# Cosine attention on one core: a third chunk of exponentials made off ScalarE, V cast for four pairs at once, twelve Q sums on TensorE, values of three pairs summed by chunk

## The chip, the cores and the metric

The kernel runs on 1 core of one Trainium2 chip. The metric is device time in microseconds (us) of one execution; lower is better. Before the change the median of 3 runs is 188.96 us (188.9 to 189.21).

## What is computed

Q, K and V have 8 batches, 12 heads, 512 rows and 64 columns, in float32; tau is 0.1.

```python
Q_norm = Q / (np.linalg.norm(Q, axis=-1, keepdims=True) + 1e-10)
K_norm = K / (np.linalg.norm(K, axis=-1, keepdims=True) + 1e-10)
scores = np.einsum('bhqd,bhkd->bhqk', Q_norm, K_norm) / tau
weights = np.exp(scores - np.max(scores, axis=-1, keepdims=True))
weights = weights / (np.sum(weights, axis=-1, keepdims=True) + 1e-10)
return np.einsum('bhqk,bhkd->bhqd', weights, V).astype(np.float32)
```

The scores lie between -10 and 10, so the kernel takes the exponentials without subtracting the maximum; the quotient is the same.

## The kernel before

The 96 heads are worked off as 48 **pairs** of heads, numbered s = 0 to 47. The 512 keys of a head are cut into 4 **chunks** c of 128. For each pair the work goes like this:

- SP (the DMA queue) loads Q, K (L311) and V (L314) into rings of buffers and stores the output (L565).
- POOL squares Q and K (L337, `sq`). The squares are summed over the 64 columns in one of two ways. For K of most pairs PE multiplies them by an identity in eight matmuls that add up in the columns 320 to 383 of an output bank (L354, op `SSQ`), and DVE reduces the 64 columns that are left to 8 (L361). For Q, and for K of pairs 35, 39, 43 and 47, DVE reduces all 512 columns (L365). Which way is taken follows from `BY_VECTOR` and `Q_ON_PE` (L626, L627) in `on_pe`.
- DVE makes 1/norm of a group of pairs by Newton steps on small tiles (L389 to L403, op `NEW`); groups have 1, 2 and, from pair 20 on, 4 pairs.
- Q is scaled on DVE, K on POOL or, for the pairs in `K_ON_DVE` (L628), on DVE (both L420, op `SCL`).
- PE transposes the scaled tiles into one PSUM tile (L426, `TR`), and DVE copies it to SBUF (L434, `EVA`). The next pair's transposes wait for that copy.
- For each chunk PE makes the scores of both heads, 128 keys by 512 queries each (L508, `SCO`), in one of two halves of the score tile `scps`, and ScalarE takes the exponential of both heads in one instruction of 1024 elements (L531, `EXP`). The scores of a chunk wait for the exponential of the chunk two before it, which read the same half.
- POOL casts V to bf16 (L536, `VC`) into `vb`, which has a 65th column of ones, so that the value matmuls give the sum of the weights too.
- PE multiplies the exponentials with V, 4 matmuls for each of 4 query tiles and 2 heads (L548, `PV`), into one bank per head; DVE takes the reciprocal of the sums (L559, `RCP`) and multiplies (L561, `NRM`). A bank is free for the next pair's values when that is done, and when the sum of squares that borrowed the bank has been reduced (`bank_free`).

Two chunks do without ScalarE: chunk 3 of pairs 37 and 45 (`OFF`, L617). Their Q scales get another factor (L411), PE makes the scores in the transposes' tile (L468, `SCX`), and a polynomial does the rest: per head two DVE steps (L473, L475), then on 1024 elements four POOL steps (L479, L480) and two DVE steps (L486, L480).

Every instruction is an `Op` with a due time and a list of what it needs. The order in which an engine issues its operations isn't made in the kernel: `ORDER` (L654 to L746) is a list of numbers for each engine, each the place at which the operation was added. Each engine is served strictly in that order, and an operation that waits holds up all behind it on its engine. `RINGS` (L631) gives the number of buffers, in this order: Q/K, V, squares, scaled tiles, transposed tiles, exponentials, outputs, norms.

The last pair (`last`, L567) is cut finer: its chunk 3 has three exponentials, and its values are made chunk by chunk (L576) in three pieces.

Of the kernel before, what the change touches and what calls it, by code (L numbers as in the profile page):

```python
# [19 lines left out]
class Program:  # L20
# [5 lines left out]
    def add(self, key, eng, kind, due, needs, emit, **kw):  # L26
        assert key not in self.ops, key
        op = Op(key, eng, kind, due, needs, emit, **kw)
        self.ops[key] = op
        self.list.append(op)  # L30
        return op

# [76 lines left out]
def bass_cosine_similarity_attention_kernel(  # L109
# [10 lines left out]
    NT = SEQ // 128  # L120
# [9 lines left out]
    qk = [sb(f"qk{i}", [128, 2, 2, NT * DIM], f32) for i in range(R_QK)]  # L130
    vf = [sb(f"vf{i}", [128, 2, NT * DIM], f32) for i in range(R_V)]
    vb = sb("vb", [128, R_QK, NT, 2, DIM + 1], bf16)
    sq = [sb(f"sq{i}", [128, 16, DIM], bf16) for i in range(R_SQ)]
    qn = [sb(f"qn{i}", [128, 2, NT, 2, DIM], bf16) for i in range(R_QN)]
# [16 lines left out]
    o_ps = [nc.alloc_psum_tensor(f"ops{b}", [128, 512], f32) for b in range(2)]  # L151
# [25 lines left out]
    def key(name, s, *rest):  # L177
# [9 lines left out]
        vb[:, :, :, :, DIM : DIM + 1].rearrange("p r c h o -> p (r c h o)"), 1.0))  # L187
# [25 lines left out]
    for s, w in sorted(((s, w) for s in range(NP) for w in range(2) if on_pe(s, w)), key=lambda j: (due_red(j[0]), j)):  # L213
# [12 lines left out]
    for s in range(NP):  # L226
        for h in range(2):
            bank_free[s, h] = before[h]
            before[h] = [("NRM", s, h)] + ([("RED",) + attached[s, h]] if (s, h) in attached else [])
# [67 lines left out]
    def pair(s):  # L297
# [6 lines left out]
        for w, x in ((0, Q), (1, K)):  # L304
            if s == 0:
# [8 lines left out]
              lambda e: e.dma_start(out=vf[iv][:, :, :], in_=src(V, s)), slot=f"v{iv}")  # L314
# [99 lines left out]
        for w in range(2):  # L414
# [3 lines left out]
            P.add(("SCL", s, w), "dve" if dve else "pool", "sclq" if dve else "sclk", T0 - (2.85 if w and not dve else 2.55) - slack(s, M_SCL),  # L418
                  [("NEW", g, (7 if direct_r(g) else 6) if acts and dve else 6 + w + (dve and w))] + ([("UNIT", s)] if s in off_of and w == 0 else []) + ([("TR", 0, w, 0), ("TR", 0, w, 1)] if s == R_QN else [key("TR", s - R_QN, w)]),
                  lambda e, w=w, r=r: e.tensor_tensor(  # L420
                      out=qn[iqn][:, w].rearrange("p t h d -> p h t d"),
                      in0=qk[iq][:, w].rearrange("p h (t d) -> p h t d", t=NT), in1=r, op=ALU.mult))
# [71 lines left out]
    def rest(s):  # L494
# [3 lines left out]
        for c in range(NT):  # L498
# [26 lines left out]
            for hs in ((0,), (1,)) if s == 0 and c < 2 else ((0, 1),):  # L525
# [9 lines left out]
        P.add(("VC", s), "pool", "vc", T0 + 3.0 - slack(s, M_VC), [("LV", s), key("PV", s - R_QK, 0, NT - 1), key("PV", s - R_QK, 1, NT - 1), "vone"],  # L535
              lambda e: e.tensor_scalar(  # L536
                  out=vb[:, iq, :, :, 0:DIM].rearrange("p c h d -> p h c d"),
                  in0=vf[iv][:, :, :].rearrange("p h (c d) -> p h c d", c=NT),
                  scalar1=1.0, scalar2=1.0, op0=ALU.mult, op1=ALU.mult))
# [3 lines left out]
        for h in range(2):  # L543
            for i in range(NT):
                def pv(e, h=h, i=i):
                    for c in range(NT):
                        t = i
                        last = e.matmul(  # L548
                            out=o_ps[h][:, 65 * t : 65 * t + 65],
                            lhsT=et[iet][:, c, h, 128 * t : 128 * t + 128], rhs=vb[:, iq, c, h, :],  # L550
                            start=(c == 0), stop=(c == NT - 1))
                    return last

                need, due = sum((exps(s, c) for c in range(NT)), []), T0 + PERIOD + 0.9 * PV_AT[4 * h + i] + late(s)
                P.add(("PV", s, h, i), "pe", "pv", due, need + [("VC", s)] + (bank_free[s, h] if i == 0 else [("PV", s, h, i - 1)]), pv)
            grid = o_ps[h][:, 0 : 65 * NT].rearrange("p (t x) -> p t x", x=65)
            P.add(("RCP", s, h), "dve", "rcp", T0 + PERIOD + 0.9 * PV_AT[4 * h + 3] + late(s),
                  [("PV", s, h, NT - 1), ("SSQ",) + attached[s, h] if (s, h) in attached else None, key("NRM", s - R_O, h)],
                  lambda e, h=h, grid=grid: e.reciprocal(out=rd[io][:, h, :], in_=grid[:, :, DIM]))  # L559
            P.add(("NRM", s, h), "dve", "nrm", T0 + PERIOD + 0.2 + 0.9 * PV_AT[4 * h + 3] + late(s), [("RCP", s, h), key("ST", s - R_O)],  # L560
                  lambda e, h=h, grid=grid: e.tensor_tensor(  # L561
                      out=ob[io][:, h], in0=grid[:, :, 0:DIM],
                      in1=rd[io][:, h, :].unsqueeze(2).to_broadcast([128, NT, DIM]), op=ALU.mult))
# [3 lines left out]
    def last(s, T0):  # L567
        iq, iet, io = s % R_QK, s % R_ET, s % R_O
        spare = t_ps[:, :, :, :].rearrange("p w t x -> p (w t x)").bitcast(f32)
        for k, (h, lo, hi) in enumerate(PIECES):  # L570
            bank = spare if k == 2 else o_ps[h]
            for c in range(NT):
                def pv(e, h=h, lo=lo, hi=hi, c=c, bank=bank):
                    for t in range(lo, hi):
# [3 lines left out]
                            rhs=vb[:, iq, c, h, :], start=(c == 0 and t == lo), stop=(c == NT - 1), skip_group_check=True)  # L578
                    return last

                op = P.add(("PV", s, k, c), "pe", "pv" if hi - lo == NT else "pvh", T0 + 0.9 * c + 2.5 + 0.1 * k,
                           [("EXP", s, c, k) if c == NT - 1 else ("EXP", s, c), ("VC", s)]
                           + (([("EVA", s)] if k == 2 else bank_free[s, h]) if c == 0 else [("PV", s, k, c - 1)]), pv)
# [33 lines left out]
OFF = {(45, 3): ((45, 45), False), (37, 3): ((37, 37), False)}  # L617
# [7 lines left out]
PE_BOTH = 4  # L625
BY_VECTOR = (35, 39, 43, 47)  # L626
Q_ON_PE = ()  # L627
K_ON_DVE = (1, 2, 3, 4, 9, 15, 21, 27, 33, 39, 40)  # L628
# [151 lines left out]
```

## Time and profile before

| | |
|---|---|
| median of 3 runs | 188.96 us (188.9 to 189.21) |
| the profiled execution | 188.88 us, span 187.0 us, granted clock 0.996 |
| HBM read, written | 37.75 MB, 12.58 MB |

The span reaches from the first to the last instruction. The costliest groups are these; the number after x is the count, then come busy time in us, the mean time of one in ns, and the engine's idle time just before them:

| line, engine | what | count | busy us | mean ns |
|---|---|---|---|---|
| L531 ACT | exponential, 128x1024 | 187 | 171.9 | 1168 |
| L337 POOL | squares, 128x1024 | 44 | 82.8 | 1897 |
| L508 PE | scores, 64x512 | 380 | 74.9 | 386 |
| L548 PE | values, 128x65 | 1504 | 73.7 | 194 |
| L561 DVE | output | 94 | 38.6 | 417 |
| L420 DVE | scale, 128x512 | 58 | 38.4 | 675 |
| L420 POOL | scale, 128x512 | 36 | 37.3 | 1046 |
| L426 PE | transposes | 376 | 33.8 | 220 |
| L434 DVE | copy of the transposed pair | 47 | 32.1 | 683 |
| L365 DVE | sums of squares, 512 to 8 | 48 | 32.1 | 681 |
| L536 POOL | cast of V, 128x512 | 48 | 31.0 | 659 |
| L354 PE | sums of squares, 128x64 | 368 | 18.2 | 193 |
| L361 DVE | the rest of these sums, 64 to 8 | 40 | 8.5 | 215 |

Records of neighbours overlap on PE, ACT, DVE and POOL, so count times mean is more than the busy time: the pace of an engine is read from the distance between two starts.

### The profile page before, as it was taken

To read this page: it belongs to the slowest core of one execution; us is meant where nothing else is said; L and a number is where in the kernel's file an instruction comes from. 1 tells how busy PE (TensorE), PEld (TensorE's weight loads), DVE (VectorE), ACT (ScalarE), POOL (GpSimd) and SP (SyncE) were. 2 spreads that over 40 slices of the span, in tenths; PEclk is the share of its full clock that TensorE was granted. 3 is DMA by queue.
4 is the path that set the end of the run, shared out by engine and by line. 5 is a ranking of instruction groups with operands and counts; after the bars stand their busy time and mean duration, and the time that the engine had idled before them with its cause. 6 is when DMAs were issued, how large, how long until landed. Compare 5 with 4: busy or idle time off the path is not lost.

```text
span 187.0 us, 6631 instructions
## 1 busy us (share of the span) xinstructions
PE 173.1 (93%) x2694; PEld 108.3 (58%) x2694; DVE 172.5 (92%) x545; ACT 181.0 (97%) x214; POOL 166.8 (89%) x152
## 2 busy tenths in 40 slices
PE   6898999999999999999999999899999989999983
PEld 2555666566565665666555555566565556656652
DVE  2789999999999999999999999999999999989863
ACT  4899999999999999999999999999999999999994
POOL 4797999999999999999999999999999999796600
PEclk9999999999999999999999999999999999999998
DMA  5999999899999998899999999896997551303315
GB/s 172 339 357 352 348 357 321 279 322 344 379 378 377 330 325 269 274 336 277 359 381 380 380 361 296 272 274 206 293 297 247 176 168 60 110 6 112 116 60 170
DMA packets 52446, 50.76 MB, mean 272 GB/s; under 512 B 3136, under 2 KB 52416, under 8 KB 52416
## 3 DMA queue, kind: packets, MB, share of 16 engines
q1 hardware_dynamic: 51984, 50.02, 81.6%
q8 instruction: 21, 0.34, 0.7%
q10 hardware_dynamic: 432, 0.33, 0.5%
q14 instruction: 9, 0.07, 0.1%
HBM read 37.75 MB, written 12.58 MB: 269 GB/s over the span
## 4 chain that ended last, share of the span: by engine, by line
ACT 92%; DMA 2%; PE 2%; SPq 1%; issue 1%; DVE 0%
ACT et L531 91%; DMA qk<-in_Q_dram 2%; PE ops L548 1%; PE ops L576 1%; PE scps L508 1%; SPq L311 0%; SPq L308 0%; ACT ys L379 0%; DVE ob L598 0%; ACT sq L329 0%; ACT nps L382 0%; PE tps L576 0%; DVE rd L587 0%
## 5 line engine op out<-in xcount | busy, mean ns | idle before, releaser
L531 ACT ACTIVATE et<-scps 128x1024 bf16<-128x1024 f32 (+1 forms) x191 | 174.0, 1155 | 0.0
L337 POOL TENSOR_TENSOR sq<-qk 128x1024 bf16<-128x1024 f32 x44 | 82.8, 1897 | 1.4 <-DMA qk<-in_K_dram 0.9
L508 PE MATMUL scps<-qt 64*128 64x512 bf16 x380 | 74.9, 386 | 8.0 <-ACT et L531 5.1
L548 PE MATMUL ops<-vb,et 128*128 128x65 bf16 x1504 | 73.7, 194 | 0.3 <-ACT et L531 0.3
L548 PEld LDWEIGHTS ops<-vb,et 128*128 128x128 bf16 x1504 | 55.9, 98 | 28.2 <-issue 20.2
L561 DVE TENSOR_TENSOR ob<-ops,rd 128x256 f32<-128x256 f32 x94 | 38.6, 417 | 0.5
L420 DVE TENSOR_TENSOR qn<-qk,nps 128x512 bf16<-128x512 f32 x58 | 38.4, 675 | 0.4 <-ACT nps L382 0.4
L420 POOL TENSOR_TENSOR qn<-qk,rk 128x512 bf16<-128x512 f32 x36 | 37.3, 1046 | 1.3 <-DVE rk L394 1.1
L508 PEld LDWEIGHTS scps<-qt 64*128 64x128 bf16 x380 | 18.8, 92 | 26.9 <-ACT et L531 14.0
L426 PE MATMUL tps<-ident,qn 128*128 128x128 bf16 x376 | 33.8, 220 | 0.4 <-POOL qn L420 0.2
L434 DVE COPY qt<-tps 128x1024 bf16<-128x1024 bf16 x47 | 32.1, 683 | 1.7 <-PE tps L426 1.4
L365 DVE TENSOR_REDUCE nps<-sq 128x8 f32<-128x512 bf16 x48 | 32.1, 681 | 0.0
L536 POOL TENSOR_SCALAR vb<-vf 128x512 bf16<-128x512 f32 x48 | 31.0, 659 | 0.2
L426 PEld LDWEIGHTS tps<-ident,qn 128*128 128x128 bf16 x376 | 21.5, 98 | 11.3 <-issue 5.7
L354 PE MATMUL ops<-sq,ident 128*128 128x64 bf16 x368 | 18.2, 193 | 0.0
L559 DVE RECIPROCAL rd<-ops 128x4 f32<-128x4 f32 x94 | 15.6, 172 | 2.7 <-PE ops L548 2.2
L354 PEld LDWEIGHTS ops<-sq,ident 128*128 128x128 bf16 x368 | 13.7, 98 | 3.6 <-issue 2.7
L361 DVE TENSOR_REDUCE nps<-ops 128x8 f32<-128x64 f32 x40 | 8.5, 215 | 0.3 <-PE ops L354 0.2
L390 DVE SCALAR_TENSOR_TENSOR nps<-nps,ys 128x32 f32<-128x32 f32 (+1 forms) x30 | 6.3, 209 | 0.3
L389 DVE TENSOR_TENSOR nps<-nps,ys 128x32 f32<-128x32 f32 (+1 forms) x30 | 6.2, 207 | 0.2
L480 POOL TENSOR_TENSOR xz<-xz 128x1024 f32<-128x1024 f32 x2 | 3.8, 1894 | 2.1 <-DVE xz L475 2.1
L191 PE MATMUL ops<-warm_in,ident 128*128 128x512 bf16 x8 | 3.5, 615 | 1.4 <-POOL ident L181 1.4
(62 smaller groups left out, 63.6 us busy)
## 6 DMA issues: line engine op xcount, KB each, us to landing
vf<-in_V_dram SPq DMA_DIRECT2D x48, 256.0 KB, 5.7
qk<-in_Q_dram SPq DMA_DIRECT2D x47, 256.0 KB, 4.5
qk<-in_K_dram SPq DMA_DIRECT2D x47, 256.0 KB, 5.6
out_dram<-ob SPq DMA_DIRECT2D x47, 256.0 KB, 3.6
qk<-in_Q_dram SPq DMA_DIRECT2D x2, 128.0 KB, 2.7
qk<-in_K_dram ACTq DMA_DIRECT2D x2, 128.0 KB, 3.0
out_dram<-ob SPq DMA_DIRECT2D x1, 128.0 KB, 1.7
out_dram<-ob ACTq DMA_DIRECT2D x1, 64.0 KB, 1.7
```

The costliest lines, as they stand in the source:

```text
L337: lambda e: e.tensor_tensor(out=sqf, in0=data, in1=data, op=ALU.mult))
L354: last = e.matmul(out=o_ps[bank][:, 320:384], lhsT=ident[:, :], rhs=sq[iqs][:, 8 * w : 8 * w + 8, 8 * k : 8 * k + 8], start=(k == 0), stop ...
L365: lambda e, w=w, dst=dst: e.tensor_reduce(out=dst, in_=sq[iqs][:, 8 * w : 8 * w + 8, :], axis=AX.X, op=ALU.add))
L420: lambda e, w=w, r=r: e.tensor_tensor(out=qn[iqn][:, w].rearrange("p t h d -> p h t d"), in0=qk[iq][:, w].rearrange("p h (t d) -> p h t d" ...
L426: last = e.transpose(t_ps[:, w, t, :], qn[iqn][:, w, t].rearrange("p h d -> p (h d)"), ident[:, :])
L434: lambda e: e.tensor_copy(out=qt[iqt][:, :, :, :].rearrange("p w t x -> p (w t x)"), in_=t_ps[:, :, :, :].rearrange("p w t x -> p (w t x)")))
L508: last = e.matmul(out=sc_ps[:, 2 * b + h, :], lhsT=qt[iqt][64 * h : 64 * h + 64, 1, c, :], rhs=qt[iqt][64 * h : 64 * h + 64, 0, :, :], sta ...
L531: lambda e, c=c, b=b, hs=hs: e.activation(out=et[iet][:, c, hs[0] : hs[-1] + 1, :], in_=sc_ps[:, 2 * b + hs[0] : 2 * b + hs[-1] + 1, :], f ...
L536: lambda e: e.tensor_scalar(out=vb[:, iq, :, :, 0:DIM].rearrange("p c h d -> p h c d"), in0=vf[iv][:, :, :].rearrange("p h (c d) -> p h c ...
L548: last = e.matmul(out=o_ps[h][:, 65 * t : 65 * t + 65], lhsT=et[iet][:, c, h, 128 * t : 128 * t + 128], rhs=vb[:, iq, c, h, :], start=(c = ...
L559: lambda e, h=h, grid=grid: e.reciprocal(out=rd[io][:, h, :], in_=grid[:, :, DIM]))
L561: lambda e, h=h, grid=grid: e.tensor_tensor(out=ob[io][:, h], in0=grid[:, :, 0:DIM], in1=rd[io][:, h, :].unsqueeze(2).to_broadcast([128, N ...
```

## The change

- `OFF` gets chunk 3 of pair 31: it leaves ScalarE and takes the way of pairs 37 and 45.
- The value matmuls of pairs 45, 37 and 31 (`BY_CHUNK`) are ordered by chunk: each `PV` operation takes one chunk for all four query tiles, the off-engine chunk last, in place of one query tile with all four chunks. The values of pairs 37 and 31 take their banks after those of the next pair (`LATER`).
- V is laid out by head, then chunk, and cast for several pairs in one instruction: pairs 8 to 15 two by two, pairs 16 to 47 four by four (`JOINT`, `join`); pairs 0 to 7 stay single.
- The Q sums of squares of the even pairs 24 to 46 go to PE (`Q_ON_PE`).
- K of pairs 23, 24, 26, 28 and 30 is scaled on DVE, K of pair 40 on POOL again (`K_ON_DVE`).
- The rings for Q/K, V, scaled tiles and outputs change from 15, 10, 4, 8 to 16, 12, 6, 6.
- All of `ORDER` is new. ScalarE's list only loses the one exponential. In the new list of PE, 8 value matmuls stand between the scores of chunks 1 and 2 of pair 47, and 32 between those of chunks 2 and 3. The stores of pairs 31 and up stand behind the last load in SP's list.

The code also gets forms for joint scales, reciprocals and outputs, which `JOINT` doesn't name; they are cut here, as is `ORDER`.

```diff
+    def join(self, name, members, eng, kind, due, needs, emit, *rest):
+
+        op = self.add((name, members[-1]) + rest, eng, kind, due, needs, emit)
+        for s in members[:-1]:
+            self.ops[(name, s) + rest] = op
...
-    vf = [sb(f"vf{i}", [128, 2, NT * DIM], f32) for i in range(R_V)]
-    vb = sb("vb", [128, R_QK, NT, 2, DIM + 1], bf16)
+    vf = sb("vf", [128, R_V, 2, NT * DIM], f32)
+    vb = sb("vb", [128, R_QK, 2, NT, DIM + 1], bf16)
...
-    for s in range(NP):
+    for s in sorted(range(NP), key=lambda i: i + (1.5 if i in LATER else 0)):
         for h in range(2):
             bank_free[s, h] = before[h]
...
-        P.add(("VC", s), "pool", "vc", T0 + 3.0 - slack(s, M_VC), [("LV", s), key("PV", s - R_QK, 0, NT - 1), key("PV", s - R_QK, 1, NT - 1), "vone"],
-              lambda e: e.tensor_scalar(
-                  out=vb[:, iq, :, :, 0:DIM].rearrange("p c h d -> p h c d"),
-                  in0=vf[iv][:, :, :].rearrange("p h (c d) -> p h c d", c=NT),
-                  scalar1=1.0, scalar2=1.0, op0=ALU.mult, op1=ALU.mult))
+        wide = {4: "v4", 2: "v"}
+        last_of = [n for n in wide if (s, wide[n]) in JOINT]
+        both = [s - i for i in range(last_of[0] - 1, -1, -1)] if last_of else [s]
+        if last_of or not any((s + i, wide[n]) in JOINT for n in wide for i in range(1, n)):
+            P.join("VC", both, "pool", {1: "vc", 2: "vc2", 4: "vc4"}[len(both)], T0 + 3.0 - slack(s, M_VC),
+                   [("LV", i) for i in both] + [key("PV", i - R_QK, h, NT - 1) for i in both for h in range(2)] + ["vone"],
+                   lambda e: e.tensor_scalar(
+                       out=vb[:, iq + 1 - len(both) : iq + 1, :, :, 0:DIM].rearrange("p r h c d -> p (r h c) d"),
+                       in0=vf[:, iv + 1 - len(both) : iv + 1].rearrange("p r h (c d) -> p (r h c) d", c=NT),
+                       scalar1=1.0, scalar2=1.0, op0=ALU.mult, op1=ALU.mult))
...
                     for c in range(NT):
                         t = i
+                        if s in BY_CHUNK:
+                            t, c = c, last_chunk[i]
                         last = e.matmul(
                             out=o_ps[h][:, 65 * t : 65 * t + 65],
-                            lhsT=et[iet][:, c, h, 128 * t : 128 * t + 128], rhs=vb[:, iq, c, h, :],
-                            start=(c == 0), stop=(c == NT - 1))
+                            lhsT=et[iet][:, c, h, 128 * t : 128 * t + 128], rhs=vb[:, iq, h, c, :],
+                            start=(i == 0 and t == 0) if s in BY_CHUNK else c == 0,
+                            stop=(i == NT - 1) if s in BY_CHUNK else c == NT - 1, skip_group_check=s in BY_CHUNK)
...
-OFF = {(45, 3): ((45, 45), False), (37, 3): ((37, 37), False)}
+OFF = {(37, 3): ((37, 37), False), (45, 3): ((45, 45), False), (31, 3): ((31, 31), False)}
...
+LATER = (37, 31)
+BY_CHUNK = (45, 37, 31)
+JOINT = ((11, 'v'), (13, 'v'), (15, 'v'), (19, 'v4'), (23, 'v4'), (27, 'v4'), (31, 'v4'), (35, 'v4'), (39, 'v4'), (43, 'v4'), (47, 'v4'), (9, 'v'))
 BY_VECTOR = (35, 39, 43, 47)
-Q_ON_PE = ()
-K_ON_DVE = (1, 2, 3, 4, 9, 15, 21, 27, 33, 39, 40)
+Q_ON_PE = (24, 26, 28, 30, 32, 34, 36, 38, 40, 42, 44, 46)
+K_ON_DVE = (1, 2, 3, 4, 9, 15, 21, 23, 24, 26, 27, 28, 30, 33, 39)
 VLAG = 3
 LATE, LATE_TO = 0.0, 10
-RINGS = 15, 10, 6, 4, 4, 4, 8, 3
+RINGS = 16, 12, 6, 6, 4, 4, 6, 3
```

## The prediction, made before the changed kernel ran

> **What bounds the kernel now.** I read the busy line of the page first, then the busy time by stretch, then the chain that ended last, then the waits of each engine, and at last the timeline of PE.
>
> ```profile
> PE 173.1 (93%) x2694; PEld 108.3 (58%) x2694; DVE 172.5 (92%) x545; ACT 181.0 (97%) x214; POOL 166.8 (89%) x152
> ```
> ```profile
> 14.00:88.00 74.00, 71.51 (x1169) 45.95 (x1168) 72.40 (x250) 74.00 (x83) 72.91 (x64) 1.00 1.01 331
> 88.00:172.00 84.00, 78.71 (x1224) 48.70 (x1219) 81.96 (x247) 83.98 (x93) 80.00 (x69) 1.00 0.75 244
> 172.00:187.00 15.00, 11.42 (x200) 7.60 (x198) 9.58 (x28) 12.21 (x17) 3.82 (x3) 0.95 0.35 116
> ```
>
> The columns of the second fence are window, length, then busy time of PE, PEld, DVE, ACT, POOL, the granted clock and the DMA. ScalarE never rests between 14 and 172 us. But DVE has only 2.0 us free in the 84 us from 88 on, PE 5.3 and POOL 4.0: all four engines are close to full where the change works (pairs 23 to 47).
>
> ```profile
> 14.77 149.41 ACT et L531 x163
> ...
> 179.94 0.39 PE scps L508 x2
> 180.33 0.84 PE ops L548 x24
> 181.17 0.32 PE scps L508 x2
> 181.50 0.59 PE ops L548 x16
> 182.09 0.32 PE scps L508 x2
> ```
>
> The chain is exponentials, one after another, and only the last 4 us go through PE. 149.41 over 163 is 0.917 us for one. In the trace's single records most starts lie 0.90 to 0.91 apart (median 0.904) though the row says 1.17 for each: neighbours overlap. The starts that are later than 0.904 add up to 2.3 us in the run. So ScalarE does stall a little, in gaps too short to be counted as idle; the place to see why is PE's timeline, where L508 makes the scores that an exponential reads:
>
> ```profile
> 155.12 0.39 PE L508 MATMUL scps<-qt 64*128 64x512 bf16 x2
> 155.44 0.66 PE L548 MATMUL ops<-vb,et 128*128 128x65 bf16 x16
> 155.93 0.40 PE L354 MATMUL ops<-sq,ident 128*128 128x64 bf16 x8
> 156.26 0.39 PE L508 MATMUL scps<-qt 64*128 64x512 bf16 x2
> ```
>
> Two score steps should be 0.904 apart; here 16 value matmuls and 8 sums of squares stand between them and they are 1.14 apart, and the exponential after them starts 1.10 after the one before it. A second kind of stall is a wait for data. Of those two matter late in the run: a transpose on PE that waited 0.23 for a scale on POOL (the exponential came 0.26 late) and value matmuls that waited 0.30 for an exponential (0.14 late).
>
> ```profile
> PE ops L548 <- ACT et L531: 0.3, 1, 0.3
> PE tps L426 <- POOL qn L420: 0.2, 1, 0.2
> ```
>
> **The change, part by part.** The profiled execution took 188.88 us with a span of 187.0 (1.9 around it, taken as fixed); the median of the runs is 188.96. The sum is made against 188.88. Durations are start to start of neighbouring records where the engine didn't wait.
>
> *ScalarE.* One exponential less (pair 31, chunk 3): -0.90.
>
> *DVE.* The chunk needs four steps of 0.61 (L473, L475), one of 1.15 (L486), one of 0.61 (L480) and a small one (L411, 0.1): +4.3. K scales move here for pairs 23, 24, 26, 28, 30 and leave for 40: four times 0.595 = +2.4. Twelve Q sums become L361 reductions of 0.131 in place of L365's 0.593: -5.5. Net +1.2. It isn't spread evenly: up to pair 34 it is +3.0 (five scales) +4.3 -2.8 (six sums) = +4.5, and it comes back later. What hides it is DVE's lead: the copy of the transposed pair (L434) ends 0.9 to 7 us before the pair's first exponential. In the new order list the work ahead of that copy grows by 1.9 for pair 34 (lead now 4.1), by 0.3 for pair 40 (lead 0.9). With ScalarE 0.9 earlier, pair 40's is 0.3 late. I take +0.2; ends 0 and +1.4 (rival C).
>
> *POOL.* The chunk: two steps of 1.85 and two of 1.0, +5.7. Four scales of 1.005 go: -4.0. Casts of V: 48 become 8 single, 4 double, 8 fourfold, so 28 instructions go. What a fourfold cast takes no row shows. The fixed part of a POOL instruction can be worked out from rows: squares start 1.852 apart at 1024 elements (L337) and 1.003 at 512 (L331), so 0.155 doesn't scale; 28 times that is -4.4. The ends are 0 and, if a cast of 2048 went as fast as one of 512 (0.585), -16; I take -4.4, from the nearest row. Net -2.7. POOL isn't what ScalarE waits for, but the wait of 0.23 above goes: the K scale of pair 43 has 2.9 us less work ahead of it. The gap with the 0.30 wait is filled in another way. Together -0.4 (0.26 and 0.14); ends 0 and -0.6.
>
> *PE.* Twelve times eight sums of squares, 29 ns apart: 12 times 0.232 = 2.8 us of work, beside the 5.3 us free from 88 on. That it fits in total isn't enough: it must fit between score steps. A score step takes 0.319, and the first one after other matmuls starts 0.126 after the last of them, where these follow each other in 0.030 (L548), 0.029 (L354) or 0.056 (L426). So a gap has room for 0.904 - 0.319 - 0.126 = 0.46 us. I counted the other work in each gap of both lists (four value matmuls 0.12, four transposes 0.224, eight sums 0.232). Up to the last pair, gaps with 0.68 us or more: 7 before, spread over the run; 17 after, all from pair 24 on. The 7 cost 0.48 now (0.05, 0.09, 0.04, 0.20, 0.12, and two nothing), 0.07 each. Ten more at 0.07 are +0.7; at 0.12, as they now come close behind each other and lateness is carried over, +1.2; at nothing, 0. I take +0.8.
>
> The 0.126 agrees with the Trainium skill, TensorEngine Tiling (Array Packing), Key Properties: changing the tiling mode drains TensorE; the trace has it at both ends of every score step (64 rows against 128).
>
> *The tail.* Now 24 value matmuls stand before the scores of chunk 2 of pair 47 and 16 before chunk 3; the latter start 2.1 us after those of chunk 1. In the new list it is 8 and 32: chunk 2's scores must wait 0.9 for their bank, then 0.319 + 0.97 + 0.126 follow: 2.3. +0.2; ends 0 and +0.3.
>
> *Values by chunk, larger rings, loads.* By-chunk sums are as many matmuls with other starts, and let pair 31's wait for its off-engine chunk alone. SP issues the same loads, and rings of 16 and 12 let them start earlier; stores of pairs 31 to 47 queue behind the last loads, and a ring of 6 needs the store of pair s before the output of s+6, some 20 us later. 0, hidden by a lead of POOL's squares of over 20 us; without that cover each load costs its 4.5 to 5.7 us to landing.
>
> **Sum:** -0.90 + 0.2 - 0.4 + 0.8 + 0.2 = -0.1: 188.8 us.
>
> **Rivals.**
>
> B, PE has the room. Crowded gaps cost little because PE catches up in light ones (two of the 7 cost nothing). For: 5.3 us free. Against: a lost start can't be won back, as ScalarE has no slack. -0.90 - 0.4 + 0.2 + 0.2 and 0 to 0.4 for the gaps: 188.0 to 188.4.
>
> C, DVE becomes the bound round pairs 31 to 37. Its 2.0 us free in that window face +1.2 of work and 0.9 less time. It decides when the lead of the copy (2.2 at pair 32) is gone: 4.5 of extra work less 2.2 lead less 0.9 free leaves 1.4 on ScalarE's path in place of the 0.2: 190.0. Against: only 1.9 of the 4.5 is listed ahead of pair 34's copy; sums of squares, 20 us ahead, can slip.
>
> D, the casts gain nothing, fourfold ones costing four single ones: POOL is +1.7 in place of -2.7, the scale of 43 is late as now or later, and the 0.4 isn't won: 189.2 to 189.8.
>
> E, DVE is locked out. Two more DVE steps with both inputs in SBUF (L486, L480) run beside POOL; if each waited for a POOL step of 1.85, DVE would lose up to 3.7 and the time be up to 192. Against: the two L486 in the trace took 1.23 and the L480 0.69 beside a busy POOL, so none waited.
>
> The Trainium skill, SBUF — State Buffer, Who interferes with whom, states an exclusive lock for that pair of operations. The trace doesn't show it here.
>
> **How the numbers follow.** Forecast 0.36, B 0.36, C 0.20, D 0.06, E 0.02. What a measurement of this kernel can tell from no change is about 0.2%, 0.38 us: the forecast's own spread, 188.6 to 189.3, counts as the same, B as faster, C, D and E as slower. The range 188.0 to 189.9 takes in all of B, the gaps' and waits' ends, D, and leaves out the upper half of C, E, and a tail below.
>
> **What would show it.** Fewer exponentials (187 to 186 of 1024 elements) with starts still 0.904 apart; the sum of late starts at 3 us or more, most behind crowded gaps from pair 24 on (forecast), or near 2 (B). Waits of PE for DVE's copy or scales near 118 to 140 us would be C. A fourfold cast near 1.9 us confirms POOL's term, 2.3 is D. L486 beyond 1.3 us is E. The forecast is wrong if late starts pile up at one place rather than in many small steps.

## The result, and the profile after

The changed kernel took 190.05 us (median of 8 runs, 189.29 to 190.24), the kernel before beside it 189.00 (8 runs, 188.82 to 189.75): a ratio of 1.0044, 95% interval 1.0026 to 1.0062. Two more sets of the unedited changed kernel, told below, gave 189.68 and 189.56, ratios 1.0049 and 1.0031. So the change makes the kernel slower by about 0.4%, where 188.8 was forecast, with 188.0 to 189.9 as the range; the first set lies above it, the two copies inside its upper end. All three sets together, without disturbed runs, have a median of 189.69 (31 runs) against 189.07 (54 runs): 0.62 us to account for.

The profiled execution of the changed kernel took 189.29 us, its fastest of the first set, with a span of 187.3 against 187.0. Its busy line, and the busy time by stretch (columns as in the prediction):

```profile
PE 177.2 (95%) x2790; PEld 113.5 (61%) x2790; DVE 173.6 (93%) x556; ACT 180.6 (96%) x213; POOL 164.7 (88%) x124
```
```profile
14.00:88.00 74.00, 72.12 (x1176) 46.84 (x1175) 72.32 (x251) 74.00 (x83) 71.91 (x53) 1.00 1.01 333
88.00:172.00 84.00, 81.41 (x1310) 52.39 (x1307) 82.79 (x255) 83.58 (x92) 77.11 (x50) 1.00 0.73 243
172.00:187.30 15.30, 11.50 (x202) 7.73 (x202) 9.97 (x30) 12.21 (x17) 5.88 (x4) 1.00 0.33 108
```

From 88 us on DVE has 1.2 us free (2.0 before), PE 2.6 (5.3 before), and POOL 6.9 (4.0 before): what POOL gained, it did not pass on. ScalarE now rests 0.42 us in this stretch (0.02 before). The chain that ended last was exponentials one after another; now it leaves them between 118 and 168 us and runs mostly through DVE:

```profile
14.84 102.67 ACT et L551 x112
117.95 0.75 PE ops L575 x20
119.81 0.60 DVE xp L493
...
154.02 1.43 DVE et L506
156.06 0.54 PE ops L575 x12
...
166.80 0.61 PE tps L446 x8
167.78 12.03 ACT et L551 x13
```

The casts cost what the prediction took: columns are count, busy time, mean ns, and idle time before.

```profile
L561 POOL TENSOR_SCALAR vb<-vf 128x2048 bf16<-128x2048 f32 x8 | 15.2, 1902 | 0.2
L561 POOL TENSOR_SCALAR vb<-vf 128x512 bf16<-128x512 f32 x8 | 4.9, 623 | 0.1
```

Start to start a cast takes 0.583 us for 512 elements, 1.010 for 1024 and 1.863 for 2048, so some 0.155 us of each instruction doesn't scale. But look where POOL's time went, in its waits (total us, times, longest):

```profile
POOL qn L440 <- DVE rk L403: 2.6, 5, 0.7
POOL sq L346 <- DMA qk<-in_K_dram: 2.3, 5, 0.7
...
POOL sq L346 <- DVE rd L593: 1.6, 1, 1.6
```

The first two were 1.1 and 0.9 us before, the third 0.3. The scale of K of pair 43, which the prediction expected sooner, shows what came of it, before and after:

```profile
159.94 1.05 POOL L420 TENSOR_TENSOR qn<-qk,rk 128x512 bf16<-128x512 f32 x1
```
```profile
162.46 1.04 POOL L440 TENSOR_TENSOR qn<-qk,rk 128x512 bf16<-128x512 f32 x1
```

POOL was busy for 151.9 us up to that scale (154.1 before), but it starts 2.5 us later, since POOL stood 4.7 us longer ahead of it. The squares of pairs 46 and 47 end 2.7 and 3.3 us later than before.

Below, (s,c) is the exponential of chunk c of pair s. The table splits each profiled execution by its exponentials: the sum of starts later than 0.904 us after the start before them (by pairs), the time from the first exponential of pair 47 to the end of the last, and from there to the end of the span.

| kernel | late, pairs 2-23 | 24-35 | 36-47 | sum | last exponentials | to the end |
|---|---|---|---|---|---|---|
| before | 0.94 | 0.55 | 0.80 | 2.29 | 3.98 | 3.27 |
| after | 0.93 | 0.86 | 1.25 | 3.04 | 4.33 | 3.39 |
| after, first copy | 0.96 | 0.88 | 1.24 | 3.08 | 4.32 | 3.60 |
| after, second copy | 1.28 | 0.98 | 1.23 | 3.49 | 4.32 | 3.66 |

The mean of the three, less the row of before: late starts +0.91, last exponentials +0.34, end +0.28. With 0.92 us for the chunk taken off (measured below) that is +0.61, against 0.62 between the medians. The start of pair 1's exponentials varies from run to run by 0.6 us, in both kernels alike, and is left out.

The late starts can also be sorted by the work that PE's list puts into the gap ahead of their scores, with the prediction's own weights. Before, the 7 gaps of 0.68 us or more (crowded gaps, below) hold 0.49 of the 2.29. After, there are 16 such gaps (the prediction counted 17), and they hold 1.44 of the 3.04; in the two copies 1.40 and 1.55. All other late starts together are 1.80 before and 1.60 after, 1.68 and 1.94 in the copies.

The largest late start that all three profiles of the changed kernel share is (41,0), 0.34 us. PE's timeline there, and DVE's:

```profile
155.44 0.39 PE L528 MATMUL scps<-qt 64*128 64x512 bf16 x2
156.06 0.54 PE L575 MATMUL ops<-vb,et 128*128 128x65 bf16 x12 [0.23 <-DVE ob L596]
156.54 0.39 PE L528 MATMUL scps<-qt 64*128 64x512 bf16 x2
156.96 0.42 PE L575 MATMUL ops<-vb,et 128*128 128x65 bf16 x8
157.22 0.63 PE L363 MATMUL ops<-sq,ident 128*128 128x64 bf16 x16
157.78 0.39 PE L528 MATMUL scps<-qt 64*128 64x512 bf16 x2
```
```profile
153.94 1.51 DVE L506 SCALAR_TENSOR_TENSOR et<-xz,xw 128x1024 bf16<-128x1024 f32 x1
155.38 0.17 DVE L593 RECIPROCAL rd<-ops 128x4 f32<-128x4 f32 x1
155.47 0.20 DVE L370 TENSOR_REDUCE nps<-ops 128x8 f32<-128x64 f32 x1
155.58 0.42 DVE L596 TENSOR_TENSOR ob<-ops,rd 128x256 f32<-128x256 f32 x1
155.92 0.98 DVE L500 TENSOR_TENSOR et<-et,xp 128x1024 bf16<-128x1024 bf16 x1
```

PE waits 0.23 us for a scaled output (L596) to free a bank, and then 16 sums of squares stand in one gap. On DVE that output is late because the polynomial step ahead of it took 1.51 us (1.25 in the kernel before, 1.23 elsewhere here): POOL's scales of pairs 41 and 42 run beside it.

### The profile page after: what moved, and what is told of

The parts are those of the page before. It is cut to its first block, busy times and chain, and to the rows that moved or that the text cites. A ratio compares the mean times of both kernels' runs of the same rounds, so it can differ in the third digit from the quotient of the medians.

```text
span 187.3 us, 6825 instructions
## 1 busy us (share of the span) xinstructions
PE 177.2 (95%) x2790; PEld 113.5 (61%) x2790; DVE 173.6 (93%) x556; ACT 180.6 (96%) x213; POOL 164.7 (88%) x124
## 4 chain that ended last, share of the span: by engine, by line
ACT 65%; DVE 22%; PE 6%; DMA 3%; issue 2%; SPq 1%
ACT et L551 64%; DVE ob L596 4%; DVE qn L440 4%; DVE qt L454 3%; DMA qk<-in_Q_dram 3%; PE ops L575 2%; PE scps L528 2%; DVE nps L374 2%; DVE rd L593 2%; DVE et L506 1%; DVE xp L493 1%; DVE nps L370 1%; PE tps L446 1%; DVE xz L495 1%; PE ops L363 1%
## 5 line engine op out<-in xcount | busy, mean ns | idle before, releaser
L575 PE MATMUL ops<-vb,et 128*128 128x65 bf16 x1504 | 76.1, 195 | 0.5 <-DVE ob L596 0.2
L440 DVE TENSOR_TENSOR qn<-qk,nps 128x512 bf16<-128x512 f32 x62 | 40.9, 676 | 0.4 <-ACT nps L391 0.4
L596 DVE TENSOR_TENSOR ob<-ops,rd 128x256 f32<-128x256 f32 x94 | 38.8, 418 | 0.4
L440 POOL TENSOR_TENSOR qn<-qk,rk 128x512 bf16<-128x512 f32 x32 | 33.9, 1074 | 2.7 <-DVE rk L403 2.6
L561 POOL TENSOR_SCALAR vb<-vf 128x512 bf16<-128x512 f32 (+2 forms) x20 | 24.3, 1220 | 0.3
L374 DVE TENSOR_REDUCE nps<-sq 128x8 f32<-128x512 bf16 x36 | 24.2, 682 | 0.0
L363 PE MATMUL ops<-sq,ident 128*128 128x64 bf16 x464 | 22.8, 193 | 0.0
L363 PEld LDWEIGHTS ops<-sq,ident 128*128 128x128 bf16 x464 | 17.2, 98 | 4.7 <-issue 3.9
L370 DVE TENSOR_REDUCE nps<-ops 128x8 f32<-128x64 f32 x52 | 11.2, 217 | 0.2 <-PE ops L363 0.2
L500 POOL TENSOR_TENSOR xz<-xz 128x1024 f32<-128x1024 f32 x3 | 5.7, 1895 | 1.9 <-DVE xz L495 1.9
L500 POOL TENSOR_TENSOR xw<-xw 128x1024 f32<-128x1024 f32 x3 | 5.7, 1894 | 0.2
```

Of the source, the lines that this page charges most:

```text
L363: last = e.matmul(out=o_ps[bank][:, 320:384], lhsT=ident[:, :], rhs=sq[iqs][:, 8 * w : 8 * w + 8, 8 * k : 8 * k + 8], start=(k == 0), stop ...
L374: lambda e, w=w, dst=dst: e.tensor_reduce(out=dst, in_=sq[iqs][:, 8 * w : 8 * w + 8, :], axis=AX.X, op=ALU.add))
L440: lambda e, w=w, r=r: e.tensor_tensor(out=qn[iqn][:, w].rearrange("p t h d -> p h t d"), in0=qk[iq][:, w].rearrange("p h (t d) -> p h t d" ...
L561: lambda e: e.tensor_scalar(out=vb[:, iq + 1 - len(both) : iq + 1, :, :, 0:DIM].rearrange("p r h c d -> p (r h c) d"), in0=vf[:, iv + 1 - ...
L575: last = e.matmul(out=o_ps[h][:, 65 * t : 65 * t + 65], lhsT=et[iet][:, c, h, 128 * t : 128 * t + 128], rhs=vb[:, iq, h, c, :], start=(i = ...
L596: emit = lambda e, a=a, b=b, grid=grid: e.tensor_tensor(out=ob[io][:, a:b], in0=grid[:, a:b, :, 0:DIM], in1=rd[io][:, a:b, :].unsqueeze(3) ...
```

## The experiments

Ratios are to the kernel before on the same chip, with 95% intervals. `ORDER` is numbers; edits of it are given by the operations' names.

**The changed kernel again, twice.** No edit.

> The changed kernel once more, nothing edited, for a second profile: the first one is of its fastest execution (189.29, median 190.05). Theory DVE (VectorE's order is full from pair 31 on, so that transposes and value matmuls wait for its copies and outputs): 190.0, and the 0.7 us that this profile is longer lies in late starts of exponentials of pairs 32 to 44, behind waits for VectorE. Theory crowding (too much other work between two score steps on TensorE): the same late starts as in the first profile, 3.0 us in all, and 0.7 us outside the exponentials. Theory loads: the 0.7 us stands behind waits of GpSimd for loads between 80 and 130 us.

Measured: 189.68 us, 1.0049 (1.0025 to 1.0073); late starts 3.08, in the same places. The span of this profile is 0.43 us longer: 0.25 of it lie ahead of pair 1 and 0.21 in the end.

> The changed kernel unedited once more, as the copy that the others of this set are compared with on the same chip: 189.6 to 190.05 us by its two earlier medians, 1.004 to 1.005 of the kernel before, with late starts that sum to 3.0 us in the profile if the load of pair 26 lands in time, and about 0.8 more if not.

Measured: 189.56 us, 1.0031 (1.0012 to 1.0050); late starts 3.49.

**The layout of V.** First the changed kernel with padded rows, then the kernel before with the new layout.

```diff
-    vb = sb("vb", [128, R_QK, 2, NT, DIM + 1], bf16)
+    vb = sb("vb", [128, R_QK, 2, NT, DIM + 2], bf16)
```

> The changed kernel with a row of the cast V 66 elements wide in place of 65 (the 66th is not read), so that every row begins on a multiple of 4 bytes. In the changed kernel the third and fourth of four value matmuls start 32.6 ns apart, before 29.4, though they are the same matmuls; V's rows lie in another order. If the odd start of a row is what costs: back to about 29.4 or less on all four, 2 us less work on TensorE, and 0.3 to 1.0 us less time if crowding matters (189.0 to 189.7), under 0.2 us less if VectorE is the bound (189.9 to 190.1). If it is the distance of 130 bytes between two rows: still 32 to 33 ns, no change of time (190.0).

Measured: 189.61 us, 1.0042 (1.0025 to 1.0060), with the value matmuls at nearly the same pace (32.8 ns in the mean, 33.0 without the padding).

```diff
-    vb = sb("vb", [128, R_QK, NT, 2, DIM + 1], bf16)
+    vb = sb("vb", [128, R_QK, 2, NT, DIM + 1], bf16)
```

> The kernel before with nothing but V's rows laid out by head, then chunk, as in the changed kernel, each pair cast by itself. If the order of the rows costs the 3 ns, they show here on the third and fourth of four value matmuls. TensorE has 5 us free in the late stretch of this kernel: theory crowding expects 189.3 to 190.0 (against 189.0), theory DVE 188.9 to 189.2.

Measured: 189.28 us, 1.0016 (1.0001 to 1.0030), late starts 2.42. The value matmuls slow from 31.7 to 33.1 ns, as in the changed kernel (33.0): the layout, not the row's odd length, costs some 2 us of PE's work, which the prediction didn't count. The late starts grow by 0.13 only. By the ratio the layout costs 0.3 us, half of the 0.62, but its interval nearly reaches 1, so its share stays open.

**The chunk.** Chunk 3 of pair 31 goes back to ScalarE; its polynomial steps leave DVE, POOL and PE.

```diff
-OFF = {(37, 3): ((37, 37), False), (45, 3): ((45, 45), False), (31, 3): ((31, 31), False)}
+OFF = {(37, 3): ((37, 37), False), (45, 3): ((45, 45), False)}
```

> The changed kernel with chunk 3 of pair 31 back on ScalarE; all else, the new order too, stays. ScalarE gets 0.90 us of work, VectorE loses 4.3, GpSimd 5.7. Theory DVE: the late starts from pair 32 to 44 (1.75 us now, 0.78 before the change) go back below 1.0, the polynomial of pair 45 isn't late any more, and the time stays within 0.4 us of the changed kernel's or falls (189.2 to 189.8): the chunk pays nothing. Theory crowding: TensorE's lists are as full as they were, late starts stay near 3.0 us, and the time rises by 0.9 (190.6).

Measured: 191.42 us, 1.0094 (1.0061 to 1.0128), the profiled execution 190.25. The stretch from pair 1 to pair 47 is 0.92 us longer than the changed kernel's, and late starts are 3.12, against 3.04. So the chunk saves its full exponential, and taking 4.3 us off DVE round pair 31 removes no stall: rival C, as it was placed, is out.

**The tail.** The last value matmuls stand otherwise between the scores of pair 47:

```diff
-pe: ... SCO47,0  (4 values)  SCO47,1  (8 values)  SCO47,2  (32 values)  SCO47,3
+pe: ... SCO47,0  (16 of pair 45)  SCO47,1  (16 of pair 46, head 0)  SCO47,2  (16 of head 1)  SCO47,3
```

> The changed kernel with the value matmuls of the last pairs spread again as before: 16 of pair 46 between the scores of chunks 1 and 2 of pair 47, 16 between those of 2 and 3 (32 in one gap in the changed kernel). In the first profile the exponential of chunk 3 of pair 47 came 0.42 later against that of chunk 0 than before. If that place sets the end: 0.3 to 0.4 us less (189.65 to 189.75). If the end hangs on VectorE's last outputs instead: no change (190.0).

Measured: 189.76 us, 1.0040 (1.0026 to 1.0054); the last exponentials take 4.75 instead of 4.33. The edit does more than spread the 32: the last values of pair 45, which need its polynomial, now stand ahead of the scores of chunk 1. There PE waits for the last polynomial step itself:

```profile
PE ops L575 <- DVE et L500: 0.5, 1, 0.5
```

Pair 45's chunk is late: its norm is ready 2.0 us later than in the kernel before (164.1 against 162.1 us), and its last DVE step ends at 180.16 against 178.0. So the order of before doesn't suit these data. What the 32 matmuls cost by themselves this edit doesn't show; the chain of the changed kernel does in part:

```profile
180.77 0.43 DVE ob L596
...
181.25 1.19 PE ops L575 x32
```

The scores of chunk 2 start at 180.77, 0.92 after those of chunk 1. The 32 matmuls could follow 0.32 later, but start after 0.48, once an output behind pair 45's values has freed their bank. The scores of chunk 3 come 2.52 after those of chunk 1, 2.15 before.

**Less work on PE and on DVE.** In the first, the Q sums on PE leave out 7 of 8 matmuls; in the second and third (the second of the changed kernel, the third of the kernel before) the outputs of pairs 24 to 46 are scaled on 16 of 64 columns; the fourth has both cuts.

```diff
-                    for k in range(8):
+                    n = 8 if w or s < EARLY else 1
+                    for k in range(n):
```
```diff
-                        out=ob[io][:, a:b], in0=grid[:, a:b, :, 0:DIM],
+                        out=ob[io][:, a:b, :, 0:n], in0=grid[:, a:b, :, 0:n],
```

> The changed kernel with one matmul in place of eight in each of the twelve Q sums on TensorE (7/8 of these sums are left out): 2.4 us less work on TensorE between score steps, all else as it is. Theory crowding: late starts fall from 3.0 to 2.3 us or less, time 189.0 to 189.2. Theory DVE: late starts stay above 2.7, time within 0.3 us of 189.7.

> The changed kernel with the output scaling on VectorE of pairs 24 to 46 cut to 16 of 64 columns (the rest of these outputs isn't computed): about 9 us less work on VectorE from pair 24 on. Theory DVE: late starts of pairs 32 to 44 go from 1.75 to under 1.0, the polynomial of pair 45 ends 2 us earlier, and the time falls by 1.0 to 1.5 us (188.2 to 188.7). Theory crowding: the crowded gaps stay, time falls by at most 0.4 (189.3).

> The kernel before with the same cut of the output scaling, for pairs 24 to 46, as a control: what VectorE's work costs there. Theory DVE (VectorE became the bound only through the change): 188.7 to 189.0, that is next to nothing. If VectorE held the kernel before up as well: 188.0 to 188.5.

> Both cuts together: output scaling of pairs 24 to 46 on 16 of 64 columns, and one matmul of eight in the twelve Q sums (the rest of both is left out). Alone, the first took late starts from 3.0 to 2.7, the second changed nothing. If TensorE and VectorE hold the exponentials up by turns, so that relief of one shows only the other: late starts 2.0 or less, 188.2 to 188.5. If it is places of the order, not load: 2.5 or more, 188.8.

| kernel | us | ratio | late sum | 24-35 | 36-47 | last exponentials |
|---|---|---|---|---|---|---|
| fewer sums | 189.58 | 1.0012 (0.9995 to 1.0029) | 3.07 | 0.80 | 1.28 | 4.33 |
| narrow outputs | 189.06 | 0.9990 (0.9967 to 1.0012) | 2.79 | 0.88 | 0.84 | 4.17 |
| before, narrow outputs | 189.08 | 0.9988 (0.9975 to 1.0001) | 2.28 | 0.53 | 0.74 | 3.98 |
| both cuts | 189.24 | 0.9989 (0.9972 to 1.0006) | 3.41 | 0.73 | 0.90 | 4.17 |

Only 4 of the 16 crowded gaps hold a Q sum. With fewer sums the late starts behind these 4 fall from 0.64 to 0.16 us ((34,2) and (41,0) by 0.2 each), and others grow ((42,2), (42,3), (22,2), 0.35 together). The profile's sum stays, and the ratio's interval reaches "no loss" and overlaps those of the copies, so what the sums cost remains unclear. Narrow outputs, which shorten DVE's work only, remove (41,0) whole and PE's wait for L596 with it, and 0.16 us of the tail. Under that cut the changed kernel and the kernel before take the same time within the intervals. So by the times most of the loss needs DVE's full outputs late in the run; of the late starts from pair 24 on, which grew from 1.35 to 2.11 with the change, the cut takes 0.39 away. The two cuts together gain little more: 1.63 from pair 24 on, against 1.72 with this one. (In the fourth, 1.03 of the 3.41 is a single late load, below.)

**Waits taken out by order.** Each engine serves its list in order, so moves are cheap to make. In the first, two operations go ahead of one another each; in the second, 16 of PE's go to another gap; in the third, both.

```diff
-dve: ... Y31,4  RED37,1 ...     pool: ... VC11  SCL8,1 ...
+dve: ... RED37,1  Y31,4 ...     pool: ... SCL8,1  VC11 ...
```

> The changed kernel with two places of its order lists mended, no work added or left out. VectorE reduces K's sum of squares of pair 37 ahead of the polynomial step of pair 31 and not behind it: GpSimd waited 1.55 us for that (its squares of pair 43 take the buffer of pair 37). GpSimd scales K of pair 8 ahead of the double cast of pairs 10 and 11: a transpose waited for it and an exponential came 0.2 late. Theory order (single waits put into the new lists hold GpSimd and, through the norms of pairs 44 to 47, the polynomial of pair 45 up): late starts 3.0 to 2.4, that polynomial 1.0 to 1.5 us earlier, the last exponentials 0.2 to 0.3 earlier; 189.0 to 189.3. Theory DVE full: GpSimd is earlier, but VectorE isn't; late starts 2.8, 189.5.

> The changed kernel with only the order of TensorE changed: in 14 crowded gaps between score steps from pair 24 on, one or two operations go to a neighbouring light gap, so that nearly all hold 0.6 us or less. Theory crowding: late starts from pair 24 on fall from 2.1 to about 1.2, 188.9 to 189.2. Theory order: the waits for VectorE and GpSimd stay, late starts fall by 0.3 at most, 189.4.

> Both edits together. If crowding and single waits each hold a share and neither covers the other: late starts near 1.6, the time 188.2 to 188.7, under the kernel before (189.0). If one covers the other: as the better of the two alone, 189.0 to 189.3.

Measured: 192.33 us, 1.0162 (1.0119 to 1.0205); 194.92 us, 1.0287 (1.0260 to 1.0315); 196.62 us, 1.0410 (1.0369 to 1.0451). All are slower. In the second only 2 gaps of 0.68 us or more are left up to the last pair, with 0.01 us of late starts, but the sum rises to 8.48: a value matmul that is moved finds its bank not ready (PE waits 4.1 us for L596, 0.2 in the changed kernel), and the scores behind it stand. The theory that room in the gaps alone lowers the sum falls here. In the first, (7,3) went as expected, but 2.8 us appeared at (33,2) to (34,0).

**The lock.** To find where these 2.8 us came from, one pair of POOL's operations alone is exchanged:

```diff
-pool: ... Y31,3  SQ43  SQ42  SQ40 ...
+pool: ... Y31,3  SQ42  SQ43  SQ40 ...
```

> The changed kernel with two squares on POOL exchanged: that of pair 42 ahead of that of pair 43, so that POOL squares right behind its polynomial steps of pair 31 instead of waiting 1.55 us. Nothing else is moved. Theory port lock: POOL's square then runs beside DVE's last polynomial step of pair 31, as in the two slow versions, where that step took 2.16 and 2.26 us instead of 0.66 and the square 2.93 and 2.73 us instead of 1.9; the outputs of pair 32 come some 1.5 us late, its banks are free late, and the exponentials (33,2) to (34,0) lose 1.6 to 2.8 us: 191.2 to 192.5 us, ratio 1.011 to 1.018. Rival, the harm in those two came from their other moves: POOL's earlier squares cost nothing, 189.3 to 189.8 us, with DVE's step at 0.66 us.

Measured: 192.39 us, 1.0167 (1.0134 to 1.0201). Two polynomial steps of pair 31 on DVE and the squares on POOL, in this version:

```profile
127.97 1.23 DVE L506 SCALAR_TENSOR_TENSOR et<-xz,xw 128x1024 bf16<-128x1024 f32 x1
...
129.33 2.16 DVE L500 TENSOR_TENSOR et<-et,xp 128x1024 bf16<-128x1024 bf16 x1
```
```profile
128.01 7.08 POOL L346 TENSOR_TENSOR sq<-qk 128x1024 bf16<-128x1024 f32 x3
```

and in the changed kernel:

```profile
127.78 1.23 DVE L506 SCALAR_TENSOR_TENSOR et<-xz,xw 128x1024 bf16<-128x1024 f32 x1
...
129.14 0.66 DVE L500 TENSOR_TENSOR et<-et,xp 128x1024 bf16<-128x1024 bf16 x1
```
```profile
129.29 5.96 POOL L346 TENSOR_TENSOR sq<-qk 128x1024 bf16<-128x1024 f32 x3 [1.55 <-DVE rd L593]
```

The three squares take 7.08 us for 5.96. The first, begun 0.04 us after DVE's L506, takes 2.93 instead of 1.89, so it stood about 1.04 us, until L506 was nearly done; it ends at 130.94, and DVE's L500, begun at 129.33, ends at 131.49, 0.55 after that. Whichever starts first keeps the other out whole. Then PE waits for the output behind L500:

```profile
131.88 0.43 PE L575 MATMUL ops<-vb,et 128*128 128x65 bf16 x8 [1.20 <-DVE ob L596]
```

and the exponential (33,2) starts 1.42 us late. In the version with two waits taken out L500 took 2.26 us. In the changed kernel as it stands POOL waits 1.55 us for a buffer, so L500 starts first, and the square, begun 0.15 us after it, is the one that is held: 2.26 us instead of 1.89.

The rest of the 2.8 us in the version with two waits taken out comes with TensorE's clock. There PE waited 1.29 us for the output behind L500, and for 3.41 us from 132.91 on the granted clock was 0.50 (columns as in the prediction):

```profile
132.90:136.30 3.40, 3.19 (x32) 2.14 (x33) 3.37 (x9) 1.49 (x2) 3.40 (x3) 0.50 0.69 208
```

A score step takes 0.53 us in it instead of 0.32. In the profile with the two squares exchanged PE waited 1.20, the clock stayed at 1.00, and the 1.42 at (33,2) is all that is late there. So the lock costs some 1.4 us and the clock some 1.4 more where it falls. The timed runs of that version fit this: 190.87 and 191.34 us at a mean clock of 0.997 to 0.998, and 192.21 to 192.95 at 0.990 to 0.991. Of the five profiles in which PE once stands 1.19 to 1.34 us, two show the drop; of the other fifteen none does while PE works. What decides isn't shown.

The Trainium skill, SBUF — State Buffer, Who interferes with whom, says that a DVE instruction with two SBUF inputs and a GpSimd instruction that reads SBUF exclude each other, and that issue order decides who blocks. These runs agree: 0.66 against 2.16 us.

**The load of pair 26.** The timed runs of the changed kernel lie above its profiled one, and in the kernel with both cuts a load came at 77.83 us instead of 75.79 and cost 1.03. Does that happen in most runs? One version moves the scale of pair 20 ahead of the square that needs the load, one moves the load ahead in SP's list, one exchanges the squares.

```diff
-pool: SQ24 SQ26 SCL20,1 SQ25 ...
+pool: SQ24 SCL20,1 SQ26 SQ25 ...
```
```diff
-sp: ... LD25 ST14 LV23 LD26 ...
+sp: ... LD25 LD26 ST14 LV23 ...
```
```diff
-pool: SQ24 SQ26 SCL20,1 SQ25 ...     VC11 SCL8,1 ...
+pool: SQ24 SQ25 SQ26 SCL20,1 ...     SCL8,1 VC11 ...
```

> The changed kernel with one step moved in POOL's order: the K scale of pair 20 stands ahead of the square of pair 26 instead of behind it. Nothing else differs, and the whole computation is done. Theory load: in the changed kernel the square of pair 26 starts about 0.7 us after its load has landed (76.50 against 75.79 us in the profile), the scale of pair 20 waits behind it, and in a run in which the load lands 1 to 2 us later (77.83 us in the profile of the version with both cuts) the exponentials of pairs 19 and 20 start some 0.8 to 1.0 us late. It expects the scatter upward to go: a median of about 189.1 to 189.4 us, close to the fastest runs of the changed kernel, 0.3 to 0.7 us under the unedited copy beside it, and no late start at (19,3) and (20,0) in the profile. Rival, the load has nothing to do with the median: the same time as the unedited copy within 0.2 us.

> The changed kernel with the two loads of pair 26 moved in SP's queue, from behind the store of pair 14 and the V load of pair 23 to ahead of both. POOL's order is the changed kernel's. The store waits for the scaled outputs of pair 14 and has held the loads behind it; ahead of it they are issued some 1 to 2 us sooner. Theory load: the square of pair 26 gets 1 to 2 us more margin, with the same effect as moving the scale: a median 0.3 to 0.7 us under the unedited copy, without a late start at (19,3) and (20,0). Rival: the same time as the unedited copy within 0.2 us.

> The changed kernel with two moves in POOL's order alone: the square of pair 25 ahead of that of pair 26, and the K scale of pair 8 ahead of the double cast of pairs 10 and 11. The version with the scale of pair 20 moved showed that it is the square of pair 25 that decides at (20,0): TensorE's sum of that square stands in its queue ahead of the first scores of pair 20, and waited 0.7 us once the square ended 1.6 us later than in the changed kernel. Theory order: with the square of pair 25 1.9 us sooner a late load can no longer reach TensorE, and the late start at (7,3) goes: 0.2 to 0.4 us off the changed kernel, 189.2 to 189.5 us (its three medians were 190.05, 189.69 and 189.56), a ratio of 1.001 to 1.002, with runs over 190 us gone but for the head's scatter. Rival: what lifts the median over the profiled run lies elsewhere (the head and the last stores), so 189.5 to 189.9 us, ratio 1.003 to 1.004.

Measured: 190.51 us, 1.0074 (1.0052 to 1.0096); 189.90 us, 1.0033 (1.0014 to 1.0052), beside the second copy's 1.0031; 190.01 us, 1.0052 (1.0032 to 1.0072). The second is the clean test: the load is issued 1.9 us sooner (in its profile it lands 0.15 sooner, at 75.64), nothing is late at (20,0), and the time is the copy's. So nothing shows the load to be what lifts the median. The first shows how thin the order is: the scale waited 1.22 us for its norm, the square of pair 25 came later, and its sum stands on PE ahead of pair 20's scores:

```profile
PE ops L363 <- POOL sq L346: 0.7, 1, 0.7
```

(20,0) started 0.90 us late. The third put the scale behind both squares and lost 0.69 at (19,3), though (7,3) went; it leaves its own question open.

**A version with five moves** was to beat both kernels: the two moves of the first two versions above, SCL8,1 ahead of VC11, SQ42 ahead of SQ43, and POOL's Y37,3 ahead of SCL40.

> The changed kernel with both moves of the two versions before it, and three more in POOL's order: the K scale of pair 8 ahead of the double cast of pairs 10 and 11, the square of pair 42 ahead of that of pair 43 (which waits 1.5 us for a DVE reduction that frees its buffer), and the last of POOL's polynomial steps of pair 37 ahead of the K scale of pair 40. DVE's and TensorE's orders are untouched. The theory that late starts come from single waits expects the late start at (7,3), 0.21 us, to go as it did in the version with two waits removed, and up to 0.3 us from the tail, since POOL reaches the squares of pairs 46 and 47 about 1 us sooner: 188.6 to 189.0 us, no slower than the kernel before. Theory tail stays: POOL's lead is lost again in the wait for the sums of pairs 44 to 47, whose last reductions keep their places on DVE and TensorE, so only the load's part and (7,3) go: 189.0 to 189.3 us. If POOL's moved squares take the SBUF port beside other DVE steps than before, new late starts may appear and eat it.

Measured: 194.90 us, 1.0282 (1.0245 to 1.0319). It has 2.8 us at (33,2) to (34,0), from the lock (L500 2.16 us) and from a clock of 0.50 for 3.41 us again, the 0.90 at (20,0), and new ones of 0.99 and 0.97 at (39,3) and (41,0). No version that was tried beats the kernel before.

## Why the prediction was wrong

The sum was -0.1 and came out as +0.61 (mean of the three profiles of the changed kernel):

| term | forecast | measured |
|---|---|---|
| ScalarE | -0.90 | -0.92 |
| waits removed and DVE (late starts outside crowded gaps) | -0.4 + 0.2 | -0.06 |
| PE (late starts behind crowded gaps) | +0.8 | +0.97 |
| tail | +0.2 | +0.34 |
| end | none | +0.28 |

**ScalarE, -0.90.** Right: 0.92.

**Waits removed, -0.4.** This is the step that failed by its mechanism. The two late starts named did go ((42,2), 0.26, and (36,1), 0.14). But the reason given, that the scale of K of pair 43 comes sooner because POOL has less work ahead of it, did not hold: it comes 2.5 us later (162.46 against 159.94). The transposes that read it still start 0.06 us after its end, now in the gap ahead of (42,3), which is 0.24 late. POOL's squares of pairs 46 and 47 are late too, so the norms of pairs 44 to 47 are 2.0 us later, and (43,2) is 0.20 late behind DVE's work that needs them. (7,3) came, 0.21, behind a scale that stands behind a double cast; it goes when the scale is put ahead. The prediction credited a wait that goes and never asked what is late next.

**DVE +0.2 and PE +0.8.** The growth lies where the prediction put it, from pair 24 on (+0.31 and +0.45 in the profiled pair) and behind crowded gaps, though by few of them: (41,0), (42,3), (34,2) and (32,1) hold 0.99 of the 1.44. But a crowded gap isn't the whole cause. At (41,0) PE also waits 0.23 for a DVE output. Thinning the sums moved late starts without lowering their sum, and spreading the crowd made it worse. Narrower DVE outputs took 0.25 off the profile's sum, and 0.41 off the late starts from pair 36 on. So DVE makes stalls of its own: not round pairs 31 to 37, as rival C had it, but behind pair 37's polynomial.

**The tail, +0.2.** 0.34. The scores of chunk 2 wait 0.92 as forecast (0.9); 0.16 more is a wait for an output that stands behind pair 45's late values, which the prediction didn't have. **The end**, from the last exponential to the end of the span, had no term, and no reason was given for that. It cost 0.28, the largest single miss: the last store takes 1.88 to 2.15 us to land, 1.76 before, while the store of pair 45 ahead of it takes 3.9 to 4.2, 3.2 before. In the versions of the changed kernel the end is anything from 3.27 to 3.92, and no edit goes with it; what slows these stores stays open.

**Loads and values, 0.** Nearly right for loads in the median; the new order's thin margins cost about 1 us when they are missed (the load of pair 26 once in the profiles). The values were taken as the same matmuls, and the layout of V makes them some 2 us longer on PE; what that costs is open, about 0.3 us by the ratio of the kernel before with the new layout.

**Rival B** falls with the 0.97 behind crowded gaps, where it had 0 to 0.4. **Rival D**, casts that gain nothing, is out (1.863 us). That its time, 189.2 to 189.8, is about the one measured is luck: the 0.4 isn't won, but not for the casts. **Rival E** was set aside because no DVE step waited in the trace before. But the lock shows there on POOL's side, at pair 37's polynomial:

```profile
149.16 1.25 DVE L486 SCALAR_TENSOR_TENSOR et<-xz,xw 128x1024 bf16<-128x1024 f32 x1
```
```profile
148.72 3.78 POOL L536 TENSOR_SCALAR vb<-vf 128x512 bf16<-128x512 f32 x4
```

Four casts in a row would take 2.4 us at their usual distance of 0.585. The second, begun 0.15 us after L486, took 1.59 instead of 0.63, and the third, behind L480, 1.05. In the changed kernel it is DVE's turn at pair 37, where L506 took 1.51 and L500 0.98; there the 0.28 us lost by L506 is more than PE's wait of 0.23. That this wait is due to the lock was read from the trace, not tried by itself.

So 0.92 us were gained on ScalarE and some 1.5 given back. How the 0.9 of late starts divide between crowded gaps, DVE's outputs, the lock and the layout of V stays open.

## What to carry to other kernels

Work taken from an engine counts only where someone waits for that engine: follow the time saved to the next wait before it is booked. Where every engine is some 90% busy and each list is served in order, an operation that comes sooner can be as harmful as one that comes late, because it meets other neighbours. Before a polynomial or any step with two SBUF inputs goes to DVE, see what POOL reads at that moment.

## What the hardware showed beyond expectation

- DVE and POOL exclude each other for whole instructions: a DVE step of 0.66 us took 2.16 to 2.26, a square of 1.89 took 2.26 to 2.93, a cast of 0.63 took 1.59. The one that is held shows a longer record and no idle time, so both engines' records must be read.
- A POOL instruction has some 0.155 us that doesn't depend on its size: casts of 512, 1024 and 2048 elements follow each other in 0.583, 1.010 and 1.863 us.
- In two executions in which PE had stood 1.2 to 1.3 us, its granted clock fell to 0.50 for 3.41 us, and a score step took 0.53 us instead of 0.32.
- In a group of four value matmuls (128x65), the step from the third to the fourth and that to the next group take 29.2 to 30 ns where the rows of V for successive chunks lie 260 bytes apart, and 32.3 to 32.6 where they lie 130 apart; padding them to 132 changes nothing. The other two steps are alike in both.
- An exponential of 1024 elements shows a duration of 1.17 us, but one comes every 0.904; taking one away gives 0.92.
